# Gathering tokens for four experts at a time instead of eight, in four visits of 128-column products

## The chip, the cores and the metric

The kernel runs on one core of a Trainium2 chip. The metric is the device time of one execution in microseconds (us). Before the change it is 835.5 us, the median of 3 runs (834.84 to 836.21). TensorE (PE) multiplies, with a weight load (PEld) ahead of each product; VectorE (DVE) and ScalarE (ACT) move and scale data, GpSimd (POOL) helps, and SyncE's queue (SP) issues the transfers from device memory.

## The reference

Two decoder layers over 256 tokens of width 1024 in float32. Each layer has a mixer (three kinds of attention, gates and an output projection) and then a mixture of experts, each with a layer norm behind it. The change is in the mixture of experts:

```python
def moe(x, router_w, router_b, w_gate, w_up, w_down):
    ...
    in_group = (jnp.arange(N_EXPERTS) // EXPERTS_PER_GROUP)[None, :] == g_star[:, None]
    _, top_idx = lax.top_k(jnp.where(in_group, sel_score, -jnp.inf), TOP_K)
    ...
    for e in range(N_EXPERTS):
        he = jax.nn.silu(xt @ w_gate[e]) * (xt @ w_up[e])
        y = y + combine[:, e:e + 1] * (he @ w_down[e])
    return y.reshape(Bn, S, D)
```

There are 16 experts with a hidden width of 512; each token uses two. One layer's expert weights are 16 x 6 MiB.

## The kernel before

**Tokens.** The 256 tokens are two tiles of 128 (t = 0, 1). Of each tile an expert gets at most CAP = 32 tokens; `onehot(r)` builds, for the eight experts of half r, the selection matrix `Sx[r]` (128 tokens x 8 experts x 2 tiles x 32 places). `gather(r)` multiplies the normed activations with it: for each of the 8 slices k of the model width and each tile t, two products (the rounded part `xh`, called x1h in the trace, and its rest `xl`, called x1l), each with a 128x128 weight load of its own and 8 x 32 = 256 moving columns, into a PSUM bank of 512 columns (`pt` for even k, `ps` for odd k). ACT (even k) or DVE (odd k) scales and shifts the bank into a slice of `xe`, the gathered tokens.

**Experts.** The loop `for p in range(NE // 2)` takes two experts at a time: `up_("g", p)` (gate, 32 instructions on PE), `up_("u", p)` (up, 32), then `down(p - 1)` (down projection of the pair before, two halves of 16), and between the two halves of `down` a function `between()`: it transposes the hidden values (`turn`, 4 products) and, from p = 3 on, adds a finished pair of experts into `acc` (`scatter`, 16 products). `gather(0)` runs in two pieces (k = 0 to 3 ahead of the first gate products, k = 4 to 7 inside them), `gather(1)` at the end of p = 3, ahead of `down(2)`. After the loop `rest()` starts the sums of the last two pairs. PE executes all of this in program order.

**Buffers.** All large tiles come from one pool of 25 buffers of 1 MiB (`slot`). Weights are loaded in 1 MiB pieces in the order of use. `pump()` issues loads as long as the weights hold fewer than `25 - target["o"]` buffers; `target["o"]` is what is kept for other tiles and follows the loop over p. `xe` takes two buffers for each half r.

Of the kernel before, what the change touches and what calls it, by code (L numbers as in the profile page):

```python
# [11 lines left out]
F32 = mybir.dt.float32  # L12
F32R = mybir.dt.float32r
I32 = mybir.dt.int32
AF = mybir.ActivationFunctionType
OP = mybir.AluOpType
# [4 lines left out]
T = 2  # L21
KD = D // 128
# [4 lines left out]
CAP = 32  # L27
# [177 lines left out]
def kernel(ctx: ExitStack, tc: tile.TileContext, x, w_in, a_w_uk, a_w_uv, c_sinks, w_branch,  # L205
# [4 lines left out]
    V, A, G, PE = (Timed(e, k, clk) for e, k in ((nc.vector, "V"), (nc.scalar, "A"), (nc.gpsimd, "G"),  # L210
                                                 (nc.tensor, "P")))
# [15 lines left out]
    target = {"o": 16}  # L227

    def slot(shape, dt, name, kind="o"):
        held[kind] += 1  # L230
        assert held["w"] + held["o"] <= nslots, (name, held)
        return big.tile(shape, dt, tag="s", name=name)

    def drop(n=1, kind="o"):
        held[kind] -= n

    def work(shape=(128, 512), dt=F32, name="wt"):
        return wk.tile(list(shape), dt, tag="w", name=name)
# [4 lines left out]
    def pmm(name="pm"):  # L243
        return pp.tile([128, 512], F32, tag="mm", name=name, bufs=4)
# [13 lines left out]
    for l in range(depth):  # L258
# [15 lines left out]
        for nm, p in moe_order:  # L274

            w, k = {"g": (moe_w_gate, 8), "u": (moe_w_up, 8), "d": (moe_w_down, 4)}[nm]
# [13 lines left out]
    def load_one(pieces=1, t=None):  # L290
        key, src, shape = loads[nxt[0]]
        nxt[0] += 1
        if t is None:
            t = slot(shape, F32, "w_" + "_".join(map(str, key)), kind="w")
        else:
            t = t.rearrange("p a b -> p (a b)")[:, :shape[1] * shape[2]].rearrange("p (a b) -> p a b", a=shape[1])
        loaded[key] = t
        if key[1:4] == ("d", NE // 2 - 1, 1):

            if key[4] == 1:  # L300
                for n in range(2):
                    for z, r in ((loaded[key[:4] + (0,)], loads[nxt[0] - 2][1]), (t, src)):
                        load(z[:, :, 512 * n:512 * n + 512], r[:, :, 512 * n:512 * n + 512])
            return
        if len(shape) == 4:
            pieces = 2
        m = shape[1] // pieces
        for i in range(pieces):
            load(t[:, m * i:m * i + m], src[:, m * i:m * i + m])

    def pump():
        while nxt[0] < len(loads) and held["w"] < nslots - target["o"]:
            load_one()

    def get(key):
        while key not in loaded:
            load_one()
        return loaded.pop(key)

    def put(n=1):  # L320
        drop(n, "w")
        pump()
# [34 lines left out]
    gpk = cpool.tile([128, DEPTH, 2, KD], F32, name="gpk")  # L357
# [622 lines left out]
    def moe(l, sc, shs, lg, rsum, zk, xh):  # L980
        target["o"] = 4
        pump()
        xl = slot([128, T, KD, 128], F32R, "x1l")
# [3 lines left out]
        def low(t, k):  # L987
            a = slice(k, k + 4)
            V.tensor_tensor(xl[:, t, a], zk[:, t, a], xh[:, t, a].bitcast(F32), op=OP.subtract)

        aff, sel = small(32, "aff"), small(64, "sel")
        z = [aff[:, NE * t:NE * t + NE] for t in range(T)]
# [56 lines left out]
        Sx = {}  # L1049
# [12 lines left out]
        xe = {}  # L1062

        def gather(r, ks=range(KD)):

            for k in ks:
                if k % 4 == 0:
                    z = slot([128, 4, 8, T, CAP], F32, "xe")
                    xe.setdefault(r, []).extend(z[:, i] for i in range(4))
                o = (ptp if k % 2 == 0 else psc)()  # L1070
                ov_ = o.rearrange("p (e t s) -> p e t s", t=T, e=8)
                for t in range(T):
                    PE.matmul(ov_[:, :, t], xh[:, t, k], Sx[r][:, :, t], start=True, stop=False)
                    PE.matmul(ov_[:, :, t], xl[:, t, k], Sx[r][:, :, t], start=False, stop=True)
                g, b = (gpk[:, l, z, k:k + 1] for z in range(2))
                if k % 2 == 0:
                    A.activation(xe[r][k], ov_, AF.Identity, bias=b, scale=g)
                else:
                    V.tensor_scalar(xe[r][k], ov_, g, b, op0=OP.mult, op1=OP.add)

        gather(0, range(4))
        low(0, 4)
        low(1, 4)
        drop()
        V.tensor_copy(pos, pc[:, 0:32])
        V.tensor_reduce(ssum, c3, axis=AX.X, op=OP.add)
        V.reciprocal(ssum, ssum)
# [57 lines left out]
        def scatter(j, h):  # L1145


            o = {(a, t): (psc, ptp)[t]() for a in range(2) for t in range(T)}
            for p in (2 * j, 2 * j + 1):
                for i in range(2):  # L1150
                    for a in range(2):
                        for t in range(T):
                            g = group(a, t)
                            PE.matmul(o[a, t], map_(p)[g], ys[p][h][i][g], start=(p % 2 == 0 and i == 0),
                                      stop=(p % 2 == 1 and i == 1))
            for a in range(2):
                for t in range(T):
                    s = xt[0][:, t, halves[h]]
                    V.tensor_tensor(s, s, o[a, t], op=OP.add)
            if h == 1:  # L1160
                drop(2)
# [43 lines left out]

        def up_(nm, p, o):
            def product(k, a, w):
                x_ = xe[p // 4][k][:, 2 * (p % 4) + a].rearrange("p t s -> p (t s)")
                PE.matmul(o[64 * a:64 * a + 64], x_, w, start=(k == 0), stop=(k == KD - 1))

            for q in range(2):
                if (nm, p, q) == ("g", 0, 0):
                    for h in range(2):
                        w = get((l, nm, p, q, h))
                        for k in range(2):
                            for a in range(2):
                                product(2 * h + k, a, w[:, a, k])
                        put()
                else:
                    w = [get((l, nm, p, q, a)) for a in range(2)]  # L1220
                    for k in range(4):
                        for a in range(2):
                            product(4 * q + k, a, w[a][:, k])
                    put(2)
                if (nm, p, q) == ("g", 0, 0):
                    gather(0, range(4, KD))
                if (nm, p, q) == ("g", 7, 0):
                    scatter(2, 0)
                if (nm, p, q) == ("u", 7, 0):
                    wt4 = over()  # L1230
                    drop(2)
                    if l + 1 < depth:
                        load_one(1, wt4)
                    else:
                        drop(1, "w")
                    clk.on = True
# [57 lines left out]
        o, parts, stm = {}, [], []  # L1294
# [89 lines left out]
        for p in range(NE // 2):  # L1384
            if p == 6:

                tc.mark_branch_hint_location(f"over{l}", engines=[mybir.EngineType.PE])
            if p == 1:
                target["o"] = 6
            if p == 2:  # L1390
                target["o"] = 7
            if p == 3:
                target["o"] = 8
            if p == 7:
                target["o"] = 16
            pg, pu = pmm(), pmm()
            up_("g", p, pg)
            if p == 1:
                slot_maps(0)
                turn(0)  # L1400
            he = hts[p] = work(name="he")
            hv, gv, uv_ = he.rearrange("p (k q) -> p q k", k=4), *(z.rearrange("p (q k) -> p q k", k=4) for z in (pg, pu))
            A.activation(hv, gv, AF.Tanh, scale=0.5)
            V.scalar_tensor_tensor(hv, hv, 1.0, gv, op0=OP.add, op1=OP.mult)
            if p == 1:
                accumulator(0)
            up_("u", p, pu)
            V.tensor_tensor(hv, hv, uv_, op=OP.mult)
            if p == 1:
                onehot(1)  # L1410
            if p == 7:
                scatter(2, 1)
            if p % 4 == 3:
                drop(2)
            if p == 3:
                gather(1)
            if p > 0:
                def between():
                    turn(p)
                    if p == 1:  # L1420
                        accumulator(1)
                    if p == 2:
                        slot_maps(1)
                        totals()
                    if p == 4:
                        stm.append(masked())
                    if 3 <= p < 7:
                        scatter((p - 3) // 2, (p - 3) % 2)
                    if p == 7:
                        parts.extend(apart())  # L1430

                down(p - 1, between)
# [34 lines left out]
```

## Time and profile before

| | before |
|---|---|
| median of 3 runs | 835.5 us |
| profiled execution | 835.41 us, of which the span from first to last instruction is 833.6 us |
| PE busy | 815.1 us |
| weight loads (PEld) busy | 503.2 us |
| DVE / ACT / POOL busy | 430.3 / 293.5 / 87.2 us |
| transferred | 265.24 MB, 318 GB/s over the span |
| granted TensorE clock | 0.997 of full speed |

The span holds mixer, experts, mixer, experts. Products are pipelined: a row's duration runs to the modelled end of its last product and overlaps the next row, so the pace of PE is read from one start to the next. What an instruction waited for is inferred from semaphores, and only for the engine's own idle time.

### The profile page before, as it was taken

The page shows a single profiled execution, that of the slowest core. Times are in us where ns is not written, and L with a number is a line of the kernel's source. Part 1 is how long each engine was busy: PE and PEld are TensorE (multiplying, and loading weights), DVE is VectorE, ACT ScalarE, POOL GpSimd, SP SyncE. Part 2 cuts the span into 40 slices and gives each one's busy share as a digit, 9 for nine tenths or more (in the row PEclk, how much of TensorE's full clock was granted, in tenths as well). Part 3 has the DMA queues.
Part 4 walks back from the last instruction along what each step waited for, and adds up shares of the span by engine and source line. Part 5 has one row for each costly group of instructions (what it writes and reads, how often), then busy time and mean ns, then how long its engine had stood idle before and what let it go on. Part 6 is the DMA issues. An engine that isn't in the chain of part 4 may idle for free.

```text
span 833.6 us, 11338 instructions
## 1 busy us (share of the span) xinstructions
PE 815.1 (98%) x4362; PEld 503.2 (60%) x4362; DVE 430.3 (52%) x895; ACT 293.5 (35%) x509; POOL 87.2 (10%) x89
## 2 busy tenths in 40 slices
PE   7999999999999999999999999999999999999996
PEld 6887778889443443333588877788884334333343
DVE  5797655785432232223489976548761422322334
ACT  5445667334311121110354476654341112111112
POOL 0222221000030000000122132110000200000001
PEclk9999999999999999999999999999999999999998
DMA  9994345986599999999899424478949999999992
GB/s 315 342 384 140 103 136 189 403 338 247 221 422 419 419 420 419 419 420 418 326 386 377 161 58 151 153 266 344 356 152 367 419 419 421 418 419 419 420 412 111
DMA packets 65691, 265.24 MB, mean 318 GB/s; under 512 B 6944, under 2 KB 11232, under 8 KB 42080
## 3 DMA queue, kind: packets, MB, share of 16 engines
q1 hardware_dynamic: 65488, 264.39, 81.2%
q8 instruction: 36, 0.59, 0.3%
q14 instruction: 23, 0.19, 0.1%
q10 hardware_dynamic: 144, 0.07, 0.0%
HBM read 263.39 MB, written 1.05 MB: 317 GB/s over the span
## 4 chain that ended last, share of the span: by engine, by line
PE 46%; DMA 5%; DVE 1%; ACT 1%; POOL 0%; POOLq 0%; issue 0%; ACTq 0%; SPq 0%
PE pm L163 38%; PE pt L163 4%; PE ps L163 3%; DMA w_u<-in_moe_w_up_dram 2%; DMA w_d<-in_moe_w_down_dram 2%; DVE acc L163 0%; DVE hl L163 0%; POOLq L1463 0%; POOL acc L163 0%; ACT zk L163 0%; DVE bm L163 0%; POOL rstd L163 0%; ACT gb L163 0%; ACT hl L163 0%; ACTq L1463 0%
## 5 line engine op out<-in xcount | busy, mean ns | idle before, releaser
L163 PE MATMUL pm<-hl,xh 128*128 128x512 f32 (+2 forms) x704 | 227.9, 390 | 1.6 <-ACT hl L163 1.3
L163 PEld LDWEIGHTS pm<-hl,xh 128*128 128x128 f32 x704 | 132.0, 190 | 29.5 <-issue 4.2
L163 PE MATMUL pm<-hl,xl 128*128 128x512 f32 (+2 forms) x352 | 134.4, 382 | 0.3 <-DVE xl L163 0.3
L163 DVE TENSOR_TENSOR hl<-w_in,hl 128x1024 fp32r<-128x1024 f32 (+2 forms) x84 | 103.2, 1238 | 60.5 <-ACT hl L163 57.9
L163 PE MATMUL pm<-w_d,he 128*64 128x512 f32 x512 | 120.1, 596 | 0.1
L163 PE MATMUL pm<-w_u,xe 128*64 128x512 f32 x512 | 117.3, 593 | 2.3 <-DMA w_u<-in_moe_w_up_dram 1.7
L163 PE MATMUL pm<-w_g,xe 128*64 128x512 f32 x512 | 116.2, 594 | 0.3 <-DMA w_g<-in_moe_w_gate_dram 0.2
L163 ACT CAST hl<-w_in 128x1024 fp32r<-128x1024 f32 (+2 forms) x86 | 84.5, 1008 | 5.6 <-DMA w_in<-in_w_in_dram 4.8
L163 PEld LDWEIGHTS pm<-w_u,xe 128*64 128x64 f32 x512 | 37.1, 137 | 78.2 <-issue 72.8
L163 PEld LDWEIGHTS pm<-w_g,xe 128*64 128x64 f32 x512 | 38.5, 137 | 71.6 <-issue 66.4
L163 PEld LDWEIGHTS pm<-w_d,he 128*64 128x64 f32 x512 | 38.0, 137 | 68.4 <-issue 64.7
L163 PEld LDWEIGHTS pm<-hl,xl 128*128 128x128 f32 x352 | 67.0, 190 | 10.5 <-DVE xl L163 1.0
L163 DVE SCALAR_TENSOR_TENSOR he<-he,pm 128x512 f32<-128x512 f32 x16 | 17.0, 1062 | 74.6 <-ACT he L163 69.6
L163 DVE TENSOR_TENSOR he<-he,pm 128x512 f32<-128x512 f32 x16 | 17.1, 1069 | 72.2 <-PE pm L163 72.2
L163 ACT COPY he<-pm 128x512 f32<-128x512 f32 x14 | 8.2, 587 | 109.7 <-PE pm L163 109.7
L163 ACT ACTIVATE he<-pm 128x512 f32<-128x512 f32 x16 | 17.2, 1075 | 80.5 <-PE pm L163 80.5
L163 PE MATMUL pm<-hl,mh 128*128 128x512 f32 (+1 forms) x160 | 45.0, 355 | 0.0
L163 DVE SCALAR_TENSOR_TENSOR yt<-pm,cs,yt 128x512 fp32r<-128x512 f32 x32 | 23.0, 748 | 42.2 <-ACT yt L163 42.2
L163 ACT ACTIVATE yt<-pm,cs 128x512 fp32r<-128x512 f32 x32 | 20.8, 686 | 66.5 <-PE pm L163 66.5
L163 PE MATMUL pm<-hl,oh 128*128 128x512 f32 x128 | 41.3, 394 | 0.0
L163 POOL TENSOR_TENSOR un<-un,su 128x512 f32<-128x512 f32 x24 | 31.0, 1297 | 94.9 <-DVE su L163 56.7
L163 POOL TENSOR_TENSOR wt<-wt 128x256 f32<-128x256 f32 (+1 forms) x36 | 27.4, 771 | 108.3 <-DVE wt L163 107.3
(199 smaller groups left out, 993.7 us busy)
## 6 DMA issues: line engine op xcount, KB each, us to landing
w_u<-in_moe_w_up_dram SPq DMA_DIRECT2D x64, 1024.0 KB, 14.5
w_g<-in_moe_w_gate_dram SPq DMA_DIRECT2D x60, 1024.0 KB, 15.7
w_d<-in_moe_w_down_dram SPq DMA_DIRECT2D x60, 1024.0 KB, 19.0
w_in<-in_w_in_dram SPq DMA_DIRECT2D x36, 1024.0 KB, 13.6
w_br<-in_w_branch_dram SPq DMA_DIRECT2D x8, 1024.0 KB, 5.1
w_wo<-in_w_o_dram SPq DMA_DIRECT2D x8, 1024.0 KB, 5.1
w_g<-in_moe_w_gate_dram SPq DMA_DIRECT2D x8, 512.0 KB, 4.0
w_d<-in_moe_w_down_dram SPq DMA_DIRECT2D x8, 512.0 KB, 17.2
```

Of the source, the lines that this page charges most:

```text
L163: r = f(*args, **kw)
```

## The change

`xe` is now gathered for four experts at a time: `gather(r)` with r = 0 to 3 uses half of `Sx[r // 2]`, and each product has 4 x 32 = 128 moving columns. Two slices k share one PSUM bank. `xe` for four experts is one buffer instead of two for eight. Visits 1, 2 and 3 stand at the end of p = 1, 3 and 5. The buffers kept for other tiles are one fewer from the first gather to p = 6, with a `pump()` behind the first piece of the gather.

```diff
         def gather(r, ks=range(KD)):
 
+            if r not in xe:
+                xe[r] = slot([128, KD, 4, T, CAP], F32, "xe")
+            es = slice(4 * (r % 2), 4 * (r % 2) + 4)
             for k in ks:
-                if k % 4 == 0:
-                    z = slot([128, 4, 8, T, CAP], F32, "xe")
-                    xe.setdefault(r, []).extend(z[:, i] for i in range(4))
-                o = (ptp if k % 2 == 0 else psc)()
-                ov_ = o.rearrange("p (e t s) -> p e t s", t=T, e=8)
+                if k % 2 == 0:
+                    o = (ptp if k % 4 == 0 else psc)()
+                z = o[:, 256 * (k % 2):256 * (k % 2) + 256]
+                ov_ = z.rearrange("p (e t s) -> p e t s", t=T, e=4)
                 for t in range(T):
-                    PE.matmul(ov_[:, :, t], xh[:, t, k], Sx[r][:, :, t], start=True, stop=False)
-                    PE.matmul(ov_[:, :, t], xl[:, t, k], Sx[r][:, :, t], start=False, stop=True)
-                g, b = (gpk[:, l, z, k:k + 1] for z in range(2))
-                if k % 2 == 0:
-                    A.activation(xe[r][k], ov_, AF.Identity, bias=b, scale=g)
+                    PE.matmul(ov_[:, :, t], xh[:, t, k], Sx[r // 2][:, es, t], start=True, stop=False)
+                    PE.matmul(ov_[:, :, t], xl[:, t, k], Sx[r // 2][:, es, t], start=False, stop=True)
+                g, b = (gpk[:, l, z_, k:k + 1] for z_ in range(2))
+                x_ = xe[r][:, k].rearrange("p e t s -> p (e t s)")
+                if k % 4 < 2:
+                    A.activation(x_, z, AF.Identity, bias=b, scale=g)
                 else:
-                    V.tensor_scalar(xe[r][k], ov_, g, b, op0=OP.mult, op1=OP.add)
+                    V.tensor_scalar(x_, z, g, b, op0=OP.mult, op1=OP.add)
 
         gather(0, range(4))
         low(0, 4)
         low(1, 4)
         drop()
+        target["o"] = 3
+        pump()
...
             def product(k, a, w):
-                x_ = xe[p // 4][k][:, 2 * (p % 4) + a].rearrange("p t s -> p (t s)")
+                x_ = xe[p // 2][:, k, 2 * (p % 2) + a].rearrange("p t s -> p (t s)")
...
             if p == 1:
+                target["o"] = 5
+            if p == 2:
                 target["o"] = 6
-            if p == 2:
+            if p == 3:
                 target["o"] = 7
-            if p == 3:
-                target["o"] = 8
...
-            if p % 4 == 3:
-                drop(2)
-            if p == 3:
-                gather(1)
+            if p % 2 == 1:
+                drop()
+                if p < 7:
+                    gather(p // 2 + 1)
```

On PE, at the start of the experts, the 16 products of the first piece (k = 0 to 3) keep their number; `pt<-cst` are transposes ahead of them and `pm<-w_g...` the first gate products behind them.

```order
 L163 MATMUL pt<-cst 128x128 x6
-L163 MATMUL pt<-Sx,x1h 128x8x32
-L163 MATMUL pt<-Sx,x1l 128x8x32
...
+L163 MATMUL pt<-Sx,x1h 128x4x32
+L163 MATMUL pt<-Sx,x1l 128x4x32
...
 L163 MATMUL pm<-w_g_0_0_1457,xe 64x512 x4
```

Each of these products has half the columns now, and stands where it stood.

On PE at the end of p = 1, between the last up products (`w_u_1_1`) and the first down products of the pair before (`w_d_0_0`), 32 products of visit 1 are put in:

```order
 L163 MATMUL pm<-w_u_1_0_1722,xe 64x512
 L163 MATMUL pm<-w_u_1_1_1724,xe 64x512
+L163 MATMUL pt<-Sx,x1h 128x4x32
+L163 MATMUL pt<-Sx,x1l 128x4x32
...
+L163 MATMUL ps<-Sx,x1h 128x4x32
+L163 MATMUL ps<-Sx,x1l 128x4x32
 L163 MATMUL pm<-w_d_0_0_1746,he 64x512
 L163 MATMUL pm<-w_d_0_1_1792,he 64x512
```

Nothing stood there before; `down(0)` and all behind it come after these 32. The same happens at p = 5, and at p = 3 the 32 products that stood there keep their number at half the columns.

On DVE at the same place, its half of the visit's scalings stands ahead of the four steps that add the shift row into `acc`:

```order
 L163 TENSOR_TENSOR he<-he,pm 128x128x4
 L163 TENSOR_TENSOR Sx<-cst,pos 128x8x32 x2
+L163 TENSOR_SCALAR xe<-ps,gpk 128x256 x4
 L163 SCALAR_TENSOR_TENSOR acc<-ps,acc 128x512 x4
 L163 SCALAR_TENSOR_TENSOR yt<-pm,cs,yt 128x512 x2
```

Four scalings of 256 columns were added there; ACT has four more at this place as well.

## Rows read from the trace of the kernel before

**Rows 1.** The page, parts 1 and 2 (GB/s in 40 slices of 20.84 us)
```profile
PE 815.1 (98%) x4362; PEld 503.2 (60%) x4362; DVE 430.3 (52%) x895; ACT 293.5 (35%) x509; POOL 87.2 (10%) x89
...
GB/s 315 342 384 140 103 136 189 403 338 247 221 422 419 419 420 419 419 420 418 326 386 377 161 58 151 153 266 344 356 152 367 419 419 421 418 419 419 420 412 111
```

**Rows 2.** Waits of the weight loads, 700 to 833 us
```profile
PEld pm L163 <- DMA w_u<-in_moe_w_up_dram: 2.7, 2, 1.6
PEld pm L163 <- DMA w_d<-in_moe_w_down_dram: 1.6, 2, 1.0
PEld pm L163 <- DMA w_g<-in_moe_w_gate_dram: 1.0, 1, 1.0
```

**Rows 3.** Timeline of PE, layer 1 (start us, us, engine line op out<-in xcount)
```profile
748.43 3.60 PE L163 MATMUL pm<-w_d,he 128*64 128x512 f32 x16
751.96 0.66 PE L163 MATMUL pm<-cst,he 128*128 128x128 f32 x4
753.68 3.65 PE L163 MATMUL pm<-w_d,he 128*64 128x512 f32 x16
757.17 7.04 PE L163 MATMUL pm<-w_g,xe 128*64 128x512 f32 x32
...
770.90 4.78 PE L163 MATMUL pm<-w_d,he 128*64 128x512 f32 x16
...
791.98 3.65 PE L163 MATMUL pm<-w_u,xe 128*64 128x512 f32 x14 [0.77 <-DMA w_u<-in_moe_w_up_dram]
795.78 4.82 PE L163 MATMUL pm<-w_u,xe 128*64 128x512 f32 x16
...
805.53 0.66 PE L163 MATMUL pt<-cst,he 128*128 128x128 f32 x4
806.12 4.47 PE L163 MATMUL pm<-w_d,he 128*64 128x512 f32 x16
810.52 0.50 PE L163 MATMUL ps<-ah,identr 128*128 128x512 f32 x1
```

**Rows 4.** Timeline of PE, layer 0, the same two places
```profile
361.73 4.49 PE L163 MATMUL pm<-w_d,he 128*64 128x512 f32 x16
...
401.27 0.50 PE L163 MATMUL ps<-ah,identr 128*128 128x512 f32 x1
```

**Rows 5.** Timeline of PE, layer 0, the three stretches of the gather and what follows
```profile
210.15 0.36 PE L163 MATMUL pt<-Sx,x1h 128*128 128x256 f32 x1
...
212.33 3.65 PE L163 MATMUL pm<-w_g,xe 128*64 128x512 f32 x16
215.91 0.39 PE L163 MATMUL pt<-Sx,x1h 128*128 128x256 f32 x1
...
218.04 3.65 PE L163 MATMUL pm<-w_g,xe 128*64 128x512 f32 x16
...
290.24 0.38 PE L163 MATMUL pt<-Sx,x1h 128*128 128x256 f32 x1
...
294.27 3.65 PE L163 MATMUL pm<-w_d,he 128*64 128x512 f32 x16
```

**Rows 6.** Small products: a tile's loads, timelines of PEld and PE
```profile
L163 PEld LDWEIGHTS pt<-comb,Sx x8: 190/192/192, 235.7 to 236.5; 128*128 128x128 f32 x8
...
235.74 0.97 PEld L163 LDWEIGHTS pt<-comb,Sx 128*128 128x128 f32 x8
...
444.53 0.61 PE L163 MATMUL pt<-uv,wt 128*128 128x128 f32 x4
444.89 0.48 PE L163 MATMUL pm<-hl,xh 128*128 128x512 f32 x1
```

**Rows 7.** Waits of SP's queue, 300 to 400 us
```profile
SPq L221 <- DMA w_u<-in_moe_w_up_dram: 25.3, 12, 2.3
...
SPq L221 <- PE pm L163: 10.5, 7, 3.1
```

**Rows 8.** The tile xe, whole span (duration ns min/median/max)
```profile
L163 DVE TENSOR_SCALAR xe<-ps,gpk x16: 809/810/811, 211.6 to 703.5; 128x512 f32<-128x512 f32 x16
```

## The prediction

> **What bounds the kernel now.** I read the page first: PE is busy for 98% of the span, and in the slices of the two expert stages the transfers run level at 418 to 422 GB/s [rows 1]. So two resources are near their limit at once, and which of them ends last has to be read stage by stage. The slices before each plateau fall to 247 and 221 GB/s (layer 0): there the buffers are full and the transfers wait for PE. From then on PE eats weights faster than they arrive: 12 MiB for two experts in one round of the loop, 22.47 us from one `down` to the next (748.43 to 770.90 [rows 3]), would need 560 GB/s. The lead melts, and near the end of each layer the weight loads wait for transfers: 2.7, 1.6 and 1.0 us, 5.3 us in five waits in layer 1 [rows 2].
>
> The waits view understates the loss, because modelled ends of products cover part of it. I therefore compare starts. From the first half of the last-but-two `down` (770.90) to `rest()` (810.52) PE needs 39.62 us in layer 1, and 39.54 us in layer 0 (361.73 to 401.27) [rows 3, 4]. The undisturbed pace of the same work: half a `down` 3.53 (748.43 to 751.96), `turn` and `scatter` 1.72, second half 3.49, gate and up together 13.73 (757.17 to 770.90), then two scatters of 1.13 (1.72 less the 0.59 of a `turn` alone, 805.53 to 806.12), then 3.53 + 0.59 + 3.49; in sum 32.34. The overflow branch in the up products takes 0.80 (3.80 from 791.98 to 795.78, where 14 products take 14/32 of half of 13.73, 3.00). What is left is 6.48 and 6.40 us; two breaks between halves are in it, for which I take 0.1 each (an estimate). So PE loses about **6.3 and 6.2 us per layer, 12.5 in all**, to transfers. That is the only slack in these stages: any work put on PE ahead of these waits is free up to this amount, if the transfers don't slip with it.
>
> **The change, part by part.** *Products.* Per layer, 64 products of 256 columns become 128 of 128 columns. The first two pieces keep 16 products each, the visit at p = 3 keeps 32, and those at p = 1 and p = 5 are new. Each product loads weights of its own. Before, the pieces took 2.18 us (210.15 to 212.33) and 2.13 us, the visit 4.03 us [rows 5]: 8.34 us per layer. Sixteen more products cost 1.88 us, so one costs 0.117 us, and 0.28 us is a break per group.
>
> What does one of 128 columns cost? By columns alone half, 0.06 us. But no load of 128x128 in the trace comes faster than about 0.11 us: eight loads for products of only 32 columns last 0.97 us, one alone 0.19, which makes (0.97 - 0.19)/7 = 0.111 us from one to the next [rows 6]. Four products of 128 columns go in 0.36 us from the first start to that of the row behind (444.53 to 444.89), 0.09 to 0.12 each [rows 6]. I take 0.111: the load is the longer half now, and halving the columns saves 0.006 us. Bounds: 0.09 below, and 0.121 (0.97/8) above.
>
> So each of three visits costs 32 x 0.111 + 0.28 = 3.83 us, each of two pieces 16 x 0.111 + 0.28 = 2.06, together 15.61 us. PE's own work grows by 15.61 - 8.34 = **7.3 us per layer** (4.6 at the lower bound, 8.5 at the upper).
>
> *Where it lies.* All of it is done by the end of p = 5, ahead of the first late transfer (`down` at 770.90 and 361.73). So it first eats the waits. For that, transfers must not be delayed by it. From 300 to 400 us SP waits 25.3 us for landings of earlier up weights alone (the pieces that must land before SP can issue more) and 10.5 us for PE [rows 7]: buffers stand free while the transfers are the bottleneck, so a PE that frees buffers later leaves them at 420 GB/s. With 7.3 us of added work against 6.2 to 6.3 of waits, all waits go and PE is the bound to the end of the layer.
>
> *One more buffer for weights.* One MiB more is loaded ahead, in the stretch where the transfers have room. At 420 GB/s that lets each layer's last transfer land 2.5 us earlier. Where PE bounds the end it is worth nothing, so I put it at zero; without the added work on PE it would be worth up to 2.5 us per layer.
>
> *Scalings.* ACT and DVE do 32 scalings of 256 columns per layer instead of 16 of 512 (0.81 us each on DVE [rows 8]). Four on each engine per visit take at most 4 x 0.81 = 3.2 us, beside 3.83 us of products, and behind each visit lies half a `down` (3.53 us [rows 3]) before PE writes those banks again. At p = 1 DVE's four stand ahead of the four shift-row steps, whose banks PE fills only after that half. Nothing on the path; if that cover failed, the last scaling's 0.8 us per visit would show, about 2 us per layer.
>
> *Sum.* 2 x 7.3 - 12.5 = +2.1 us. The profiled execution's own time is 835.4 us (span 833.6 and 1.8 around it), 0.1 below the median of the runs shown: **837.5 us**. With 0.09 us a product PE grows by 4.6, less than the waits: 2 x 4.6 - 12.5 = -3.3, 832.1 us. With 0.121 and only the 5.3 us of waits that the weight loads show [rows 2] it is 2 x (8.5 - 5.3) = +6.4, 841.8 us.
>
> **The rivals.**
>
> *Faster: products cost by columns.* If loads of rounded weights hide better than those of rows 6, a product costs 0.06 us; PE's growth is 128 x 0.06 + 5 x 0.28 - 8.34 = 0.7 us per layer, and the transfers bound the end, now with one buffer more: 2.5 us earlier in each layer, 835.4 - 5.0 = 830.4 us. The point where it decides: growth below the 6.2 us of waits, 0.103 us a product. For it: the gather's products before came 0.117 us apart, so that their loads were no visible bound at 256 columns. Against it: rows 6, whatever the columns. The Trainium skill has a rule on this side (TensorE: Matmul & The Clock Gate, section Back-to-back issue gap): in a stream of load and product pairs it gives a sustained 81 ns per product at 128 columns. By it PE would grow by about 3.4 us per layer and this rival would come true in full, also at 830.4 us (an estimate with that page's figure); the trace does not agree so far, since its nearest products stand 111 ns apart [rows 6]. I give this case 0.12.
>
> *Slower: the transfers slip with PE.* If later buffers push the stream back as much as PE, the waits stay, and the growth is paid in full: 835.4 + 2 x 7.3 = 850.0 us, about 843.8 if half of the waits stay. It would happen where the queue runs dry behind a visit: 3.83 us without a freed buffer. For it: SP's waits for PE are not zero even late, 10.5 us [rows 7]. Against it: the plateau without a dip, and the extra buffer. 0.14.
>
> *Slower by far: narrow rounded products take two turns.* The trace has no product of rounded type under 256 columns. If such a product ran in two turns of 0.111 us, PE would grow by 128 x 0.222 + 1.4 - 8.34 = 21.5 us per layer: 835.4 + 43.0 - 12.5 = 865.9 us. Nothing in the rows speaks for it but the absence. 0.08.
>
> **How the numbers follow.** The forecast (0.66) is the sum, 837.5 us, with 832.1 to 841.8 as its own range. A measurement of this kernel can tell about 0.2%, 1.7 us, from no change. The forecast stands just beyond that; of its 0.66 I put 0.03 on faster, 0.31 on no change and 0.32 on slower. With 0.12 for the faster rival and 0.22 for the slower two: faster 0.15, same 0.31, slower 0.54. The range reaches down to 830, to take in the faster rival, and up to 843, where half of the waits stay; left out are the two-turn case and half of the slipping case, 0.15.
>
> **What the changed profile would show.** Gather products of 128 columns, 256 over both layers where 128 of 256 columns stood, 0.11 us from start to start; visits of about 3.8 us at the end of p = 1, 3 and 5. In the stretch from the last-but-two `down` to `rest()` some 33.3 us instead of 39.6, and no wait of the weight loads for w_u, w_g or w_d there. The GB/s plateau should end at the same height, with a gap before the next layer's weights. The prediction is wrong if the products stand clearly off 0.11 us, if the waits for w_d and w_u are still there, or if DVE's or ACT's scalings appear as releasers of PE behind a visit.

## The result, and the profile after

The changed kernel takes **888.7 us** (median, 887.4 to 889.7) against 835.3 us before (the median of four runs): ratio 1.0636, 95% interval 1.0623 to 1.0648. That is slower by 53.4 us, where 2.2 us were forecast and 843 us was the top of the range. The profiled execution has a span of 885.9 us.

The page of the changed kernel, parts 1 and 2 (40 slices of 22.1 us; PEclk is the granted clock in tenths of full speed):

```profile
PE 847.4 (96%) x4490; PEld 523.1 (59%) x4490; DVE 434.0 (49%) x911; ACT 299.2 (34%) x525; POOL 87.3 (10%) x89
...
PEclk9999999998989989899999999999999898997999
...
GB/s 308 352 357 96 142 144 287 337 368 84 381 348 382 419 407 418 419 419 391 309 336 143 144 95 114 178 370 334 286 154 420 322 409 419 414 419 419 420 165 48
```

PE is busy for a smaller share than before [rows 1], the clock has dents in both expert stages, and the GB/s plateaus have holes (348 and 382 in the first, 322 in the second). So PE lost time in two ways: it waited, and it ran slowly.

The waits of PE over the whole span (us in total, times, longest us) name two releasers that the kernel before did not have:

```profile
PE pt L163 <- ACT xe L163: 11.8, 16, 1.2
PE ps L163 <- DVE xe L163: 10.3, 16, 0.7
```

PE waits 32 times for the scaling of `xe`: 16 times per layer, four in each full visit and two in each of the first pieces. The timeline of PE behind the first and the second piece, in the visit at the end of p = 1, and in the stretch that I had used to size the waits for transfers, in both layers:

```profile
214.51 6.12 PE L163 MATMUL pm<-w_g,xe 128*64 128x512 f32 x16
220.57 0.33 PE L163 MATMUL pt<-Sx,x1h 128*128 128x128 f32 x1
...
224.23 3.65 PE L163 MATMUL pm<-w_g,xe 128*64 128x512 f32 x16
227.71 7.04 PE L163 MATMUL pm<-w_u,xe 128*64 128x512 f32 x32
...
251.30 0.33 PE L163 MATMUL pt<-Sx,x1h 128*128 128x128 f32 x1
...
251.58 0.28 PE L163 MATMUL pt<-Sx,x1h 128*128 128x128 f32 x1
251.69 0.27 PE L163 MATMUL pt<-Sx,x1l 128*128 128x128 f32 x1
252.68 0.33 PE L163 MATMUL pt<-Sx,x1h 128*128 128x128 f32 x1 [0.71 <-ACT xe L163]
...
253.51 0.28 PE L163 MATMUL ps<-Sx,x1l 128*128 128x128 f32 x1
254.43 0.33 PE L163 MATMUL ps<-Sx,x1h 128*128 128x128 f32 x1 [0.64 <-DVE xe L163]
...
259.07 6.03 PE L163 MATMUL pm<-w_d,he 128*64 128x512 f32 x16
265.03 0.66 PE L163 MATMUL pm<-cst,he 128*128 128x128 f32 x4
...
394.26 3.60 PE L163 MATMUL pm<-w_d,he 128*64 128x512 f32 x16
...
427.59 0.50 PE L163 MATMUL ps<-ah,identr 128*128 128x512 f32 x1
...
829.74 3.60 PE L163 MATMUL pm<-w_d,he 128*64 128x512 f32 x16
...
862.86 0.50 PE L163 MATMUL ps<-ah,identr 128*128 128x512 f32 x1
```

Products next to each other stand 0.11 us apart (251.58, 251.69), as forecast. But the first product of every odd slice k starts about 1 us after the last one of the even slice (251.69 to 252.68, 253.51 to 254.43). The visit lasts 7.77 us (251.30 to 259.07) instead of 3.83. Behind it half a `down` takes 5.96 us (259.07 to 265.03), where [rows 3] has 3.53. From the last-but-two `down` to `rest()` it is 33.33 and 33.12 us, as forecast, against 39.5 and 39.6 in [rows 3, 4].

The stretches of the changed kernel (us, busy time of the engines, PEclk, DMA share, GB/s): the first piece, the gate products behind it, the second piece, the visit at p = 1, and what follows.

```profile
209.70:214.50 4.80, 2.93 (x18) 2.49 (x16) 0.87 (x3) 2.43 (x4) 0.00 (x0) 0.81 0.00 0
214.50:220.50 6.00, 6.00 (x17) 1.62 (x16) 2.29 (x7) 0.00 (x0) 0.00 (x0) 0.58 0.22 49
220.50:224.30 3.80, 2.51 (x20) 2.08 (x20) 0.54 (x1) 1.13 (x2) 0.00 (x0) 1.00 1.00 418
...
251.30:259.10 7.80, 5.16 (x36) 4.42 (x34) 3.33 (x6) 2.26 (x4) 0.00 (x0) 0.87 1.01 420
259.10:266.00 6.90, 6.90 (x26) 2.56 (x26) 0.54 (x1) 0.28 (x1) 0.00 (x0) 0.65 0.43 173
```

The granted clock is 0.58 behind the first piece, in which PE stopped twice, and 0.65 behind the visit, in which it stopped four times; a mean between 0.5 and 1 is a stretch that lay partly at the lower of the two levels, 1.2 GHz, and partly at 2.4 GHz.

The order of the built program shows where the waits come from. These are PE's rows of the second piece, with what each waits for: first the changed kernel, then the version of the second experiment. Rows 781 and 782 stand for the four products of the even slice: the pair comes once for each tile t.

```
781 L163 MATMUL pt<-Sx,x1h 128x4x32
782 L163 MATMUL pt<-Sx,x1l 128x4x32 [waits DVE_49]
783 L163 MATMUL pt<-Sx,x1h 128x4x32 [waits Activation_49]
784 L163 MATMUL pt<-Sx,x1l 128x4x32

781 L163 MATMUL pt<-Sx,x1h 128x4x32
782 L163 MATMUL pt<-Sx,x1l 128x4x32 [waits DVE_49]
783 L163 MATMUL pt<-Sx,x1h 128x4x32
784 L163 MATMUL pt<-Sx,x1l 128x4x32
```

Row 783 is the first product of the odd slice. It writes the other half of the bank that ACT reads for the even slice, and the program makes it wait for ACT, although the columns do not overlap. This stands in the program; no run here says whether the chip would need it.

### The profile page after: what moved, and what is told of

It is laid out like the page before. It is cut to its first block, busy times and chain, and to the rows that moved or that the text cites. A ratio compares the mean times of both kernels' runs of the same rounds, so it can differ in the third digit from the quotient of the medians.

```text
span 885.9 us, 11612 instructions
## 1 busy us (share of the span) xinstructions
PE 847.4 (96%) x4490; PEld 523.1 (59%) x4490; DVE 434.0 (49%) x911; ACT 299.2 (34%) x525; POOL 87.3 (10%) x89
## 5 line engine op out<-in xcount | busy, mean ns | idle before, releaser
L163 PE MATMUL pm<-w_d,he 128*64 128x512 f32 x512 | 126.9, 643 | 0.0
L163 PE MATMUL pm<-w_u,xe 128*64 128x512 f32 x512 | 113.1, 593 | 0.5 <-DMA w_d<-in_moe_w_down_dram 0.4
L163 ACT ACTIVATE xe<-pt,gpk 128x256 f32<-128x256 f32 x32 | 18.1, 564 | 78.8 <-PE pt L163 78.8
L163 DVE TENSOR_SCALAR xe<-ps,gpk 128x256 f32<-128x256 f32 x32 | 17.4, 544 | 53.4 <-PE ps L163 53.4
```

The source lines that it names most:

```text
L163: r = f(*args, **kw)
```

## The experiments

All times stand beside runs of the kernel before on the same chip: 835.6 us for the first four, 835.25 us for the last three. Three of them add transposes that nobody needs, as their texts say; none leaves work out.

**A bank for each slice.** The changed kernel with one thing undone (with the bank, ACT and DVE take turns by slice again):

```diff
-                if k % 2 == 0:
-                    o = (ptp if k % 4 == 0 else psc)()
-                z = o[:, 256 * (k % 2):256 * (k % 2) + 256]
+                o = (ptp if k % 2 == 0 else psc)()
+                z = o[:, :256]
...
-                if k % 4 < 2:
+                if k % 2 == 0:
                     A.activation(x_, z, AF.Identity, bias=b, scale=g)
```

> The changed kernel with one thing undone: each slice k gets a PSUM bank of its own again (even k pt, odd k ps), of which 256 columns are used. Theory A (two slices share a bank, so PE waits for the scaling of the first before it may write the second; these waits and the low clock behind them are the whole error): no wait of PE for ACT xe or DVE xe, visits of 3.7 to 3.9 us instead of 7.8 to 8.6, granted clock above 0.99, and the sum of the prediction comes true: 835 to 840 us, about 837.5. Theory B (the visits wait for the scalings in any case, since four banks are too few for eight slices): visits stay above 6 us, 865 us or more. Theory C (waits for transfers were not there to be eaten, the added work is paid in full): 848 to 851 us.

Measured: 836.85 us (836.22 to 838.64), ratio 1.0019, interval 1.0009 to 1.0028. This is what theory A said; B and C fall. PE's timeline of this run, the visit at p = 1 and the late stretch of layer 0:

```profile
245.10 0.33 PE L163 MATMUL pt<-Sx,x1h 128*128 128x128 f32 x1
...
245.49 0.28 PE L163 MATMUL pt<-Sx,x1l 128*128 128x128 f32 x1
245.60 0.28 PE L163 MATMUL ps<-Sx,x1h 128*128 128x128 f32 x1
...
248.97 3.65 PE L163 MATMUL pm<-w_d,he 128*64 128x512 f32 x16
252.55 0.66 PE L163 MATMUL pm<-cst,he 128*128 128x128 f32 x4
...
369.29 3.60 PE L163 MATMUL pm<-w_d,he 128*64 128x512 f32 x16
...
402.57 0.50 PE L163 MATMUL ps<-ah,identr 128*128 128x512 f32 x1
```

The next slice follows 0.11 us behind (245.49 to 245.60), the visit takes 3.87 us, the half `down` behind it 3.58, and the late stretch 33.28 us. The mean clock of the run is 0.998. This is the kernel that my sum described.

**One bank for two slices, scaled after both.** The bank is still shared; only the order of issue differs:

```diff
+                if k % 2 == 0:
+                    continue
+                for j in (k - 1, k):
...
+                    if j % 4 < 2:
+                        A.activation(x_, z, AF.Identity, bias=b, scale=g)
+                    else:
+                        V.tensor_scalar(x_, z, g, b, op0=OP.mult, op1=OP.add)
```

> The changed kernel, two slices still in one bank, but PE writes both before either is scaled, so that no write follows a reading of the same bank. Theory A: the waits go as with banks of their own, 836 to 842 us. Theory A' (sharing a bank is itself slow, whatever the order): as the changed kernel, above 875 us.

Measured: 836.52 us (835.85 to 837.02), ratio 1.0010, interval 1.0000 to 1.0019. Theory A again: PE has no wait for the scaling of `xe` in this run, though two slices still share a bank and ACT and DVE scale the same slices as in the changed kernel. So it is not the sharing that costs, but a write issued behind a reading of the same bank.

**The waits filled with transposes.**

```diff
                 if k % 2 == 0:
                     o = (ptp if k % 4 == 0 else psc)()
+                else:
+                    warm(9, pmm)
```

> The changed kernel with nine transposes of 128 columns (about 1.0 us, into a bank that nobody reads) in each place where PE waited for the scaling of the first slice, 20 places per layer... 4 in each full visit. They do no useful work. The waits stay, PE is busy in them. If the granted clock fell because PE was idle in the visits, it stays at 0.99 or above and the products behind the visits go at full pace: 888.7 less some 2 x 8 us, 868 to 876 us. If the fall has nothing to do with idleness, or the transposes cost more than they fill: 885 us or more.

(There are 16 such places per layer; the 20 in that text is a slip.) Measured: 872.2 us (871.97 to 872.38), mean clock 0.995. PE's timeline of this run, the visit at p = 1:

```profile
249.19 0.28 PE L163 MATMUL pt<-Sx,x1l 128*128 128x128 f32 x1
249.30 1.17 PE L163 MATMUL pm<-cst 128*128 128x128 f32 x9
250.22 0.31 PE L163 MATMUL pt<-Sx,x1h 128*128 128x128 f32 x1
...
256.36 3.65 PE L163 MATMUL pm<-w_d,he 128*64 128x512 f32 x16
259.94 0.66 PE L163 MATMUL pm<-cst,he 128*128 128x128 f32 x4
```

The gaps are about as long as before (249.19 to 250.22, 1.03 us), but PE is busy in them, and the half `down` behind takes 3.58 us. So the low clock came from PE's standing still.

The difference of the two times, 888.7 - 872.2 = 16.5 us, is less than the clock's price, because this version loses time in one more place. PE's timeline in its late stretch of layer 0:

```profile
384.36 3.60 PE L163 MATMUL pm<-w_d,he 128*64 128x512 f32 x16
...
407.40 5.35 PE L163 MATMUL pm<-w_u,xe 128*64 128x512 f32 x16 [2.55 <-DMA w_d<-in_moe_w_down_dram]
412.68 0.49 PE L163 MATMUL ps<-yt,st 32*128 32x512 f32 x1
...
421.57 0.50 PE L163 MATMUL ps<-ah,identr 128*128 128x512 f32 x1
```

The stretch takes 37.21 us, 3.9 more than in the first experiment (33.28); in layer 1 it takes 33.12. PE waits there for weights. Behind its longer visit at p = 1 the transfers had fallen back: from 260 to 270 us they ran at 321 GB/s, in the first experiment at 419; that this made the wait was not tried apart. The changed kernel comes to the same place 10 us later and loses only 0.36 us to a transfer there, so its low clock was worth about 16.5 + 3.9 = 20.4 us.

**The kernel before with added work.** At the end of p = 5 in each layer, useless transposes:

```diff
             if p == 3:
                 gather(1)
+            if p == 5:
+                warm(56)
```

> The kernel before with 56 transposes (6.2 us of PE, no useful work) per layer at the end of p = 5, ahead of the late transfers. If PE's waits for weights (6.2 us per layer by the prediction) can be filled with work and the transfers don't slip: 835 to 837 us. If the transfers slip with PE, or the waits are smaller than worked out: up to 848 us.

> The kernel before with 112 useless transposes (12.4 us) per layer at the end of p = 5, twice those of the earlier run. Theory A: the first 6.2 us per layer fill PE's waits for weights, the rest is paid in full: 835.5 + 2 x (12.4 - 6.2) = 847 to 849 us. If transfers slip with PE: 855 us or more.

Measured: 837.18 us with 56 (ratio 1.0020, interval 1.0011 to 1.0029) and 848.34 us with 112 (ratio 1.0158, 1.0142 to 1.0174). PE's timeline with 56:

```profile
338.69 6.33 PE L163 MATMUL pt<-cst 128*128 128x128 f32 x56
344.96 1.51 PE L163 MATMUL pm<-w_d,he 128*64 128x512 f32 x6
```

They take 6.27 us per layer, 12.5 in all; 1.6 of these show. Of the 24.7 us of 112 transposes 13.1 show. So 10.9 and 11.6 us were free: the waits for weights were there to be filled, nearly as worked out (12.5). With 56 the late stretch takes 33.29 us in layer 0, but 34.74 in layer 1, where some wait is left: there the transfers seem to have slipped a little. The first time is a little above what was expected, the second as expected.

**No extra buffer for weights.** A bank for each slice, and `target["o"]` as before the change.

> The first experiment (a bank for each slice) with the numbers of kept buffers as before the change, so that weights have no buffer more. Theory A: PE bounds both layers' ends there, so the extra buffer is worth nothing: the same as the first experiment, 836 to 838 us. Rival (the extra buffer carries part of the result): 839 us or more.

Measured: 837.39 us (836.35 to 838.30), ratio 1.0024, interval 1.0015 to 1.0033, which overlaps that of the first experiment, as theory A said. The buffer's worth there can't be told from zero.

**Two visits of four experts, one of eight.** Banks of their own; only the first eight experts are gathered in two visits, and the last eight in one of 256 columns at p = 3, into two buffers:

```diff
+            if r < 2:
...
+                es, n, m = slice(4 * r, 4 * r + 4), 4, 0
+            else:
+                w = [slot([128, 4, 8, T, CAP], F32, "xe") for i in range(2)]
...
+                es, n, m = slice(0, 8), 8, 1
...
-            if p % 2 == 1:
+            if p in (1, 3):
                 drop()
-                if p < 7:
-                    gather(p // 2 + 1)
+                gather(p // 2 + 1)
+            if p == 7:
+                drop(2)
```

> Banks of their own as in the first experiment, but only the first eight experts are gathered in two visits of 128 columns (ahead of p = 0 and at the end of p = 1); the last eight stay one visit of 256 columns at the end of p = 3, into two buffers. PE's added work is then about 3.6 us per layer by the prediction's prices (two pieces of 2.06, a visit of 3.83 and one of 4.03, 11.98, against 8.34), less than the waits for weights, and the weights still have one buffer more until p = 3. Theory A (waits for transfers are eaten by added work; below that the transfers bound the end and the extra buffer counts): 2.5 us less per layer than before, 830 to 832 us. Rival (the extra buffer brings nothing where it counts): 834 to 836 us.

Measured: **832.78 us** (832.41 to 833.25), ratio 0.9969, interval 0.9957 to 0.9981: faster than both kernels, by 0.3% against the one before, and between theory A and the rival, nearer to A. Waits of the weight loads for weights over the whole span of this run:

```profile
PEld pm L163 <- DMA w_u<-in_moe_w_up_dram: 1.7, 6, 0.3
PEld pm L163 <- DMA w_d<-in_moe_w_down_dram: 1.6, 3, 0.7
```

Its first gather product and its late stretch of layer 0, on PE's timeline:

```profile
209.57 0.30 PE L163 MATMUL pt<-Sx,x1h 128*128 128x128 f32 x1
...
364.81 3.60 PE L163 MATMUL pm<-w_d,he 128*64 128x512 f32 x16
...
399.35 0.50 PE L163 MATMUL ps<-ah,identr 128*128 128x512 f32 x1
```

The stretch takes 34.54 us, 1.3 more than in the first experiment: some wait is left. `rest()` starts 1.9 us earlier than before (401.27 in [rows 4]), but 0.6 of that is an earlier start of the gather (209.57 against 210.15 in [rows 5]). From there to `rest()` the layer is 1.3 us shorter, and so is layer 1; together that is the 2.5 us by which the kernel is faster, where 5.0 were expected. So the extra buffer seems to count where PE's work is less than its waits, at half the price I gave it. No run has these visits with the old buffers, so that it is the buffer is argued and not shown.

## Why the prediction was wrong

**The step that failed** is the one on the scalings: "Nothing on the path". I saw that two slices share a bank and that ACT and DVE have twice as many scalings, and I set their sum (3.2 us per visit) beside the products of the visit. The only cover that I looked at was the half `down` behind a visit, and I priced its failure at about 2 us per layer. But a sum says nothing of the order. With one bank for two slices, PE's write of the odd slice stands behind the reading of the even one, so products and scalings take turns inside the visit: 15.6 us of waits per layer, and a low clock on top. The built order with its waits shows it in one row (783), which stood in the program before the run.

**What stood in its place.** By differences of runs and of their timelines:

| part | from | us |
|---|---|---|
| added products, less the waits they fill | 836.85 - 835.60 | 1.3 |
| 32 waits for scalings, about 1.0 us each | all pieces and visits, filled version less first experiment: 61.74 - 30.46 | 31.3 |
| low clock in and behind the visits | the rest: 888.71 - 836.85 - 31.3 | 20.6 |
| sum | measured 53.4 | 53.2 |

The whole difference of the filled version and the first experiment, 872.20 - 836.85 = 35.4 us, is, to 0.2 us, these 31.3 and the 3.9 that only the filled version loses in its late stretch. The filler of nine transposes is a little longer than most of the waits it fills (1.03 against 0.92 to 1.00 us in the visit at p = 1), so the border between the last two parts is good to two or three microseconds.

**What was right.** A product of 128 columns costs 0.11 us (251.58 to 251.69; the same in the first experiment), the pace of the loads in [rows 6], and not half of one of 256, as the rival by columns had it. The Trainium skill's 81 ns per product at 128 columns (TensorE: Matmul & The Clock Gate, section Back-to-back issue gap) is not what this trace shows, which has 0.11 us. PE's work grew by 6.9 us per layer in the first experiment (its pieces and visits take 15.23 us), where 7.3 were forecast. The waits for transfers went: some 6.3 us per layer are gone from the late stretch, in the changed kernel and in the first experiment. With the bank undone, 836.85 us were measured where the sum gave 837.5. The rival of two turns per narrow product fell with the 0.11 us. The rival that the transfers slip with PE did not come true with visits of 3.8 us; with 56 transposes and in the filled version a part of it shows, 1.4 us in layer 1 and 3.9 us in layer 0.

**What I left out of the rivals** is this very wait, and with it the clock: the stops of PE cost 31.3 us here and the low clock that followed them another 20.6, and I had no term for either.

## What to carry to other kernels

When a change puts two results into one PSUM bank, look where the reading of the first stands against the writing of the second: write both, then read both, or give each a bank. Here either way took the waits out. A sum of hidden work is no proof that it is hidden; the waits in the built order show turns that a sum can't. And where an engine waits for transfers late in a stage, as PE did here, work put ahead of that wait can be nearly free up to its length, which a run with useless work measures directly.

## What the hardware showed that was not expected

Four stops of PE in a visit of 7.8 us, each 0.9 to 1.0 us from start to start, were followed by a stretch at a granted clock of 0.65, in which half a `down` took 5.96 us instead of 3.53; behind the first piece, with two stops of 1.44 and 0.98 us, it was 0.58, and 16 gate products took 6.06 us (214.51 to 220.57) instead of 3.58 [rows 5]. But behind the second piece, which had two stops as well, of 0.94 and 0.91 us, the same number of gate products took 3.48 us (224.23 to 227.71), the full pace; no run here says what tells the two pieces apart. In the filled version the mean clock of the run stayed at 0.995, and the one stop that it had in a late stretch, 2.55 us, was followed by 16 up products in 5.28 us (407.40 to 412.68) instead of the 3.59 of the changed kernel (415.11 to 418.70). Visits of 3.8 us without stops left the mean clock of the first experiment at 0.998.
